# Four orders, and the skip weights as a column, in a hybrid pooling and state-space layer on one core

## The chip, the cores and the metric

The kernel runs on one core of a Trainium2 chip. The core has a matrix unit (TensorE, PE in the profile, with its weight loads as PEld), a vector engine (VectorE, DVE), a scalar engine (ScalarE, ACT), a general engine (GpSimd, POOL) and an engine that mostly issues transfers (SyncE, SP). Each works through its own instructions in program order and waits on semaphores for the others. The metric is the device time of one execution in microseconds (us), as the median of several executions.

## The reference

One layer is computed for 256 positions of a new stream and 32 positions of a running one, 288 tokens in all, in fp32. In short:

```python
def run_layer(x, pos, hist_pool, hist_sconv, h0, hist_fconv, p):
    xn = rmsnorm(x, p['norm_mix_pre'])
    proj = xn @ p['w_in']
    u, z, xbc, dt_raw = proj[..., :o1], proj[..., o1:o2], proj[..., o2:o3], proj[..., o3:]
    y_pool, new_pool = pool_mixer(u, hist_pool, pos, p['w_pool'], p['pool_scale'])
    y_ssd, new_sconv, new_h = ssd_mixer(z, xbc, dt_raw, ...)
    mix = jnp.concatenate([y_pool, y_ssd], axis=-1) @ p['w_out']
    x = x + rmsnorm(mix, p['norm_mix_post'])
    hn = rmsnorm(x, p['norm_ffn_pre'])
    up, new_fconv = causal_dwconv(hn @ p['w_up'], hist_fconv, ...)
    gate, val = up[..., :D_FF], up[..., D_FF:]
    x = x + rmsnorm((jax.nn.silu(gate) * val) @ p['w_down'], p['norm_ffn_post'])
```

The model width is 2048, the inner width of the state-space mixer 2048 (32 heads of 64), the feed-forward width 5632. Two lines of the mixer matter here. Each head adds its input times a skip weight, and the old state is carried on with the decay over all positions:

```python
    y = (y_diag + y_off).reshape(b, s, G, J, P) + D[..., None] * xh
    h = dec[..., None, None] * h + st        # dec = exp of the summed decays of a chunk
```

## The kernel before

Activations lie with channels on the 128 partitions and the 288 tokens along the free axis, so a tile of 128 channels is 128x288. The 2048 channels of the model are 16 tiles. A weight tile arrives in fp32 (`raw`); ACT copies its high part (`whi`, L152) and DVE subtracts to get the low part (`wlo`, L153). Activations are split the same way (`xn`, `hn`: ACT writes the high half, DVE the low half). A product in fp32 is then three matmuls of 128x128 by 128x288: high by high, high by low, low by high (`mm3`, L166).

The stages run one after the other on PE:

- **The first chunks** (L300 to L404). The columns of `w_in` for the B, C and first x channels are taken in 11 chunks along the contraction, six of one tile of 128 channels and five of two (CHUNKS). `prepare` splits a chunk one ahead of its use; `squares(q)` (L353 on ACT, L354 on DVE) squares two tiles of x and adds them to a running sum. The table SQUARES says behind which chunk's splits which squares are issued: `{4: (0,), 5: (1,), 6: (2,), 7: (3, 4), 8: (5,), 9: (6,), 10: (7,)}`. All of this is held in program order. In the last chunk but one, after 24 of its 36 matmuls, two matmuls by a matrix of ones (L391) sum the squares over the partitions into `prs`; from that the inverse root `rstd` is made (L394, L395), which every evacuation of these products needs.
- **The x and z projections** (L822 and on), eight and eight, each of 256 columns: 96 matmuls on PE. After an x projection the accumulators are evacuated (L442), convolved (L453, L455) and passed through tanh (L459). Meanwhile dt becomes decays `g`; `ptok` holds transposes of it by token (L567) and, from two small products, the skip weight of each channel (L575: head weights spread over the partitions by a 0/1 matrix) and the last decay of each head on all partitions (L576). Both are copied to `dcol`.
- **The masks** (`ssd_masks`): for a quad of four heads, 12 ReLU instructions (L653), one exponential (L656) on ACT, and a product with C·B (L658) on DVE. `run_masks(XS_RATE[i])` issues them after projection i; before, XS_RATE is (0, 0, 1, 0, 1, 0, 0, 1). `run_pair` then issues the products of two quads (L678 to L684), after the last x projection and after three of the z projections. L694 adds the skip term, scaled by a column of `dcol`.
- **The output projection, the new state, the residual** (L880 to L1060). The new state uses the last decays on all partitions, at L1024.
- **The residual and the up projection** (L1086 on). `rm` is the inverse root for the residual norm. Each of the 16 tiles `mg` is multiplied by it (L1119, DVE) and gets x added: tiles 0 to 7 (NEAR) from a copy in memory on chip (L1121, DVE), tiles 8 to 15 by an accumulating transfer from POOL's queue (L1123). `hn_of(t)` then makes the split `hn` (L1100 on ACT, L1101 on DVE), a square (L1108, ACT) and the running sum (L1115, DVE). The program walks s from 0 to 15 and calls `hn_of` one tile behind for near tiles and eight behind for far ones. PE takes the up projection four tiles at a time.

Between pieces that are pinned, a scheduler decides the order of each engine's instructions; it is fixed when the kernel is built.

Of the kernel before, what the change touches and what calls it, by code (L numbers as in the profile page):

```python
# [1 line left out]

# [10 lines left out]
AX = mybir.AxisListType  # L13
# [26 lines left out]
XS_RATE = (0, 0, 1, 0, 1, 0, 0, 1)  # L40
# [11 lines left out]
    ("f_b", 2 * NF), ("hist_f", 2 * 2 * NF),  # L52
# [4 lines left out]
NEAR = 8  # L57
W_GAP = 48
# [11 lines left out]
def body(  # L70
# [190 lines left out]
    hp = side1.tile([HEADS, 3], F32, name="hp")  # L261
# [26 lines left out]
    id32 = ident[:HEADS, :HEADS]  # L288
# [67 lines left out]
    SQUARES = {4: (0,), 5: (1,), 6: (2,), 7: (3, 4), 8: (5,), 9: (6,), 10: (7,)}  # L356
# [3 lines left out]
    for i, (kb, n) in enumerate(CHUNKS):  # L360
# [26 lines left out]
        for q, (r, m, k, x) in enumerate(products):  # L387
            if i == len(CHUNKS) - 2 and q == 24:
# [25 lines left out]
    act.activation(g_ssd, col["ssd_norm"], AF.Copy, scale=0.5)  # L414
    start.close()
# [30 lines left out]

    def conv_out(i, e, out):
# [11 lines left out]
        act.activation(th, c, AF.Tanh)  # L459
# [104 lines left out]
    p_t = aux([P, 10 * HEADS + NX], "ptok")  # L564
    p_tok = p_t[:, : 9 * HEADS].rearrange("p (b h) -> p b h", b=3)
# [3 lines left out]
    hv = htile("hv", NX + HEADS)  # L569
    elast = htile("elast", 1)  # L570
    act.activation(elast, g[:, 415:416], AF.Exp)
# [3 lines left out]
    follow(pe.matmul(p_[:, :NX], sel64.rearrange("h r q -> h (r q)"), hv[:, :NX], start=True, stop=True))  # L575
    follow(pe.matmul(p_[:, NX:], ones[:HEADS, :], hv[:, NX:], start=True, stop=True))  # L576
# [5 lines left out]
    dcol = const.tile([P, NX + HEADS], F32, name="dcol")  # L582
    dve.tensor_copy(dcol, p_)
# [26 lines left out]
    def ssd_first(q):  # L610
# [6 lines left out]
        act.activation(ce, gb[:, :, 384:], AF.Exp)  # L617
# [14 lines left out]
    def ssd_masks(q):  # L632
# [485 lines left out]
    for s in range(KD):  # L1118
# [5 lines left out]
        while todo and todo[0] + (1 if todo[0] < NEAR else NEAR) <= s:  # L1124
            hn_of(todo.pop(0))
# [337 lines left out]
```

## Time and profile before

| | |
|---|---|
| median of 3 runs | 1305.62 us (1305.27 to 1305.78) |
| the profiled execution | 1306.34 us |
| its span in the profile | 1304.6 us |
| x projections (PE at L166 after the first stage) | from 47.49 us |
| transposes of the decays on PE | 106.20 us |
| first products of a quad on PE | 150.45 us |
| residual norm to up projection on PE | 463.7 to 467.8 us |

The timeline gives start, duration, engine, line, and after `x` the number of instructions that a row holds; brackets give the idle time before a row and what ended it. Durations of matmuls overlap, so their pace is read from one start to the next. In the view of windows, the first columns are length and each engine's busy time with its count; at the end of the row stand PE's granted clock, the DMA share and GB/s.

### The profile page before, as it was taken

The numbers are of one execution on the slowest core, as the hardware profiler recorded it, in microseconds if no ns is written. First come the engines' busy times: TensorE is split into PE (matmuls) and PEld (weight loads), VectorE is DVE, ScalarE is ACT, GpSimd is POOL, SyncE is SP. The second block draws the span as 40 slices with busy tenths as digits, with TensorE's granted clock in tenths as the row PEclk, the third lists the DMA queues.
The fourth block names the chain that finished last, engine by engine and source line by source line (L and its number), as shares of the span: only waits on it lengthen the run. The fifth ranks groups of instructions, "written<-read, shape, count | busy, mean of one in ns | idle before, by whom it ended". The sixth has DMA issues, their size and how long they took to land.

```text
span 1304.6 us, 25289 instructions
## 1 busy us (share of the span) xinstructions
PE 1296.9 (99%) x10043; PEld 1286.6 (99%) x10043; DVE 897.0 (69%) x1531; ACT 671.6 (51%) x1013; POOL 251.7 (19%) x399
## 2 busy tenths in 40 slices
PE   9999999999999999999999999999999999999998
PEld 9999999999999999999999999999999999999997
DVE  7999987989655588867766744336666666664454
ACT  7557676646544567554544433334444454444442
POOL 2343231222222231211211100001111111201110
PEclk9999999999999999999999999999999999999999
DMA  8668877445767478766545455455545555466663
GB/s 329 204 211 274 250 242 232 137 166 169 242 213 229 140 198 259 210 185 202 172 162 166 160 170 175 157 175 182 174 162 166 175 175 165 163 233 191 209 182 113
DMA packets 110326, 251.75 MB, mean 193 GB/s; under 512 B 64768, under 2 KB 73888, under 8 KB 87936
## 3 DMA queue, kind: packets, MB, share of 16 engines
q1 hardware_dynamic: 103856, 233.36, 55.7%
q0 software_dynamic: 5824, 16.13, 4.3%
q8 instruction: 78, 1.28, 0.4%
q10 hardware_dynamic: 528, 0.66, 0.2%
q14 instruction: 40, 0.33, 0.1%
HBM read 237.11 MB, written 13.00 MB: 192 GB/s over the span
## 4 chain that ended last, share of the span: by engine, by line
PE 96%; DMA 1%; DVE 1%; ACT 1%; issue 0%; SPq 0%; ACTq 0%
PE acc L166 91%; PE acc_x L166 1%; DMA raw<-in_w_first 1%; PE py L678 1%; PE acc L1324 0%; DVE w L334 0%; PE acc L1325 0%; DMA xg<-in_x_g 0%; PE acc_t L1347 0%; DVE sq L354 0%; PE py L680 0%; PE acc_x L397 0%; PE acc L397 0%; DVE xn L321 0%; PE pst L1036 0%
## 5 line engine op out<-in xcount | busy, mean ns | idle before, releaser
L153 DVE TENSOR_TENSOR wlo<-raw,whi 128x1024 fp32r<-128x1024 f32 (+1 forms) x396 | 472.7, 1196 | 297.1 <-ACT whi L152 296.1
L152 ACT ACTIVATE whi<-raw 128x1024 fp32r<-128x1024 f32 (+1 forms) x396 | 408.0, 1033 | 471.1 <-PE acc L166 381.3
L166 PE MATMUL acc<-hn,whi 128*128 128x288 f32 x2752 | 539.0, 294 | 0.5 <-ACT hn L1100 0.4
L166 PEld LDWEIGHTS acc<-hn,whi 128*128 128x128 f32 x2752 | 436.3, 188 | 1.5 <-ACT hn L1100 0.8
L166 PE MATMUL acc<-hn,wlo 128*128 128x288 f32 x1376 | 399.6, 291 | 0.0
L166 PEld LDWEIGHTS acc<-hn,wlo 128*128 128x128 f32 x1376 | 259.0, 188 | 0.0
L166 PE MATMUL acc<-fa,whi 128*128 128x288 f32 x1320 | 257.5, 293 | 0.0
L166 PE MATMUL acc<-xn,whi 128*128 128x288 f32 x1216 | 238.5, 294 | 0.0
L166 PEld LDWEIGHTS acc<-fa,whi 128*128 128x128 f32 x1320 | 208.9, 188 | 0.0
L166 PEld LDWEIGHTS acc<-xn,whi 128*128 128x128 f32 x1216 | 192.9, 188 | 0.6 <-issue 0.5
L166 PE MATMUL acc<-fa,wlo 128*128 128x288 f32 x660 | 192.1, 291 | 0.0
L166 PE MATMUL acc<-xn,wlo 128*128 128x288 f32 x608 | 177.4, 292 | 0.0
L166 PEld LDWEIGHTS acc<-fa,wlo 128*128 128x128 f32 x660 | 124.3, 188 | 0.0
L1150 POOL COPY fc_stage<-ebuf 128x4 f32<-128x4 f32 x88 | 26.9, 306 | 472.8 <-DVE ebuf L1149 451.4
L166 PEld LDWEIGHTS acc<-xn,wlo 128*128 128x128 f32 x608 | 114.5, 188 | 0.0
L166 PE MATMUL acc<-mixs,whi 128*128 128x288 f32 x512 | 100.2, 293 | 0.0
L1145 POOL COPY ebuf<-cols 128x2 f32<-128x2 f32 x88 | 71.7, 816 | 111.1 <-DVE fc L1156 91.8
L1156 DVE SCALAR_TENSOR_TENSOR fc<-ebuf,cols,fc 128x290 f32<-128x290 f32 x176 | 90.5, 518 | 3.5 <-ACT fc L1154 0.8
L1154 ACT ACTIVATE fc<-ebuf,cols 128x290 f32<-128x290 f32 x88 | 54.4, 623 | 72.4 <-DVE ebuf L1149 72.4
L166 PEld LDWEIGHTS acc<-mixs,whi 128*128 128x128 f32 x512 | 81.1, 188 | 0.0
L166 PE MATMUL acc<-mixs,wlo 128*128 128x288 f32 x256 | 74.6, 291 | 0.0
L166 PE MATMUL acc<-mixp,whi 128*128 128x288 f32 x256 | 50.1, 293 | 0.0
(323 smaller groups left out, 1245.3 us busy)
## 6 DMA issues: line engine op xcount, KB each, us to landing
raw<-in_w_up SPq DMA_DIRECT2D x80, 1024.0 KB, 5.1
raw<-in_w_in SPq DMA_DIRECT2D x38, 1024.0 KB, 5.3
raw<-in_w_down SPq DMA_DIRECT2D x32, 1024.0 KB, 5.0
raw<-in_w_out SPq DMA_DIRECT2D x22, 1024.0 KB, 5.2
raw<-in_w_down SPq DMA_DIRECT2D x16, 768.0 KB, 4.4
raw<-in_w_up SPq DMA_DIRECT2D x14, 512.0 KB, 4.6
gb<-g_d POOLq DMA_DIRECT2D x8, 832.0 KB, 6.4
raw<-in_w_first SPq DMA_DIRECT2D x5, 768.0 KB, 13.0
```

The lines of the kernel that those rows point to most:

```text
L152: act.activation(hi, raw[:, k : k + n, :], AF.Copy)
L153: dve.tensor_tensor(lo, raw[:, k : k + n, :], hi.bitcast(F32), op=ALU.subtract)
L166: ins = pe.matmul(out, w, a[:, x, :], start=start and n == 0, stop=stop and n == 2)
L678: ins = pe.matmul(y[c, 0:256], xw[:, 0, f_], m[:, h, 0:256], start=True, stop=False)
L1145: pool.tensor_copy(e[:, 258:260], hist_f[:, :, i])
L1150: pool.tensor_copy(fc_stage[:, :, :, i], e[:, 256:324].rearrange("p (s c) -> p s c", c=34)[:, :, 0:2])
L1154: act.activation(c, e[:, 0:290], AF.Identity, bias=col["f_b"][:, i : i + 1], scale=f_w[:, 0, i : i + 1])
L1156: dve.scalar_tensor_tensor(c, e[:, r_ : r_ + 290], f_w[:, r_, i : i + 1], c, op0=ALU.mult, op1=ALU.add)
```

## The change

Four orders and one piece of data are changed.

1. SQUARES becomes `{4: (0, 1), 5: (2,), 6: (3,), 7: (4,), 8: (5,), 9: (6,), 10: (7,)}`.
2. The two matmuls of the sums are issued ahead of the last chunk instead of after 24 matmuls of the one before.
3. XS_RATE becomes (0, 0, 0, 0, 0, 1, 1, 1), and the first quad's masks and decays on ACT are issued only after the last tanh recorded so far.
4. The walk over the 16 residual tiles becomes 0, 1, 2, 3, 8, 4, 9, 5, 10, 6, 11, 7, 12, 13, 14, 15, and `hn_of` is called in it only ahead of near tiles; the rest follow at the end.
5. The skip weights come as 16 more columns of `cols` (repeated 64 times per head on the host), the last decays are stored to memory as `e_d` and read back with one broadcast to `kept`, and the two small products with all that fed them are gone. The scheduler's order of ACT, DVE and SP differs around all these places.

```diff
-XS_RATE = (0, 0, 1, 0, 1, 0, 0, 1)
+XS_RATE = (0, 0, 0, 0, 0, 1, 1, 1)
...
-    ("f_b", 2 * NF), ("hist_f", 2 * 2 * NF),
+    ("f_b", 2 * NF), ("hist_f", 2 * 2 * NF), ("skip", NX),
...
+FAR_AT = 4
...
-    SQUARES = {4: (0,), 5: (1,), 6: (2,), 7: (3, 4), 8: (5,), 9: (6,), 10: (7,)}
+    SQUARES = {4: (0, 1), 5: (2,), 6: (3,), 7: (4,), 8: (5,), 9: (6,), 10: (7,)}
...
-            if i == len(CHUNKS) - 2 and q == 24:
+            if i == len(CHUNKS) - 1 and q == 0:
...
+    skip = col["skip"]
...
-    sel = mp.tile([HEADS, 2], F32, name="sel")
-    pick = mp.tile([HEADS, NX], F32, name="pick")
-    sel64 = mp.tile([HEADS, 2, 64], F32, name="sel64")
-    with tc.issue_after(last_split[1].ins):
-        dve.tensor_reduce(sel, id32.rearrange("h (t r) -> h r t", r=2), axis=AX.X, op=ALU.add)
-        dve.tensor_reduce(pick, id32.rearrange("h (t r) -> h t r", r=2), axis=AX.X, op=ALU.add)
-        dve.tensor_copy(sel64, sel.unsqueeze(2).broadcast_to([HEADS, 2, 64]))
...
-        act.activation(th, c, AF.Tanh)
+        tanhs.append(act.activation(th, c, AF.Tanh))
...
-    hv = htile("hv", NX + HEADS)
     elast = htile("elast", 1)
     act.activation(elast, g[:, 415:416], AF.Exp)
-    dve.tensor_scalar(hv[:, 0:NX], pick, hp[:, 2:3], None, op0=ALU.mult)
-    dve.tensor_scalar(hv[:, NX:], id32, elast, None, op0=ALU.mult)
-    p_ = p_t[:, 9 * HEADS :]
-    follow(pe.matmul(p_[:, :NX], sel64.rearrange("h r q -> h (r q)"), hv[:, :NX], start=True, stop=True))
-    follow(pe.matmul(p_[:, NX:], ones[:HEADS, :], hv[:, NX:], start=True, stop=True))
+    e_d = dram.tile([HEADS, 1], F32, name="e_d")
+    sp.dma_start(out=e_d, in_=elast)
...
-    dcol = const.tile([P, NX + HEADS], F32, name="dcol")
-    dve.tensor_copy(dcol, p_)
...
-        act.activation(ce, gb[:, :, 384:], AF.Exp)
+        with ExitStack() as order:
+            if not q:
+                order.enter_context(tc.issue_after(tanhs[-1].ins))
+            act.activation(ce, gb[:, :, 384:], AF.Exp)
...
-                    if exps:
-                        order.enter_context(tc.issue_after(exps[-1].ins))
+                    order.enter_context(tc.issue_after((exps or tanhs)[-1].ins))
...
-                dve.scalar_tensor_tensor(o, o, dcol[:, t : t + 1], y, op0=ALU.mult, op1=ALU.add)
+                dve.scalar_tensor_tensor(o, o, skip[:, t : t + 1], y, op0=ALU.mult, op1=ALU.add)
...
+    kept = const.tile([P, HEADS], F32, name="kept")
+    sp.dma_start(out=kept, in_=e_d.rearrange("h o -> o h").broadcast_to([P, HEADS]))
...
-            w = dcol[:, NX:][:, heads]
+            w = kept[:, heads]
...
-    for s in range(KD):
+    turns = list(range(FAR_AT))
+    for near, far in zip_longest(range(FAR_AT, NEAR), range(NEAR, KD)):
+        turns.extend(t for t in (far, near) if t is not None)
+    for s in turns:
...
-        while todo and todo[0] + (1 if todo[0] < NEAR else NEAR) <= s:
+        while todo and todo[0] < s < NEAR:
             hn_of(todo.pop(0))
...
-    "heads": np.stack([v[n][0] for n in ("ssd_dt_bias", "ssd_a_log", "ssd_d")], axis=1),
+    "heads": np.stack([v[n][0] for n in ("ssd_dt_bias", "ssd_a_log")], axis=1),
```

How the instructions move is seen in the order of each engine's program. First PE around the sums of squares, before (`prs`, fed by `sq_r`, between rows of the last two chunks; the 16 rows of `w_dt` follow them):

```order
L397 MATMUL acc<-xn,w 128x288 x24
L391 MATMUL prs<-sq_r,ones_r 128x288 x2
L397 MATMUL acc_x<-xn,w 128x288 x12
L397 MATMUL acc<-xn,w 128x288 x24
L397 MATMUL acc_x<-xn,w 128x288 x12
L404 MATMUL acc<-xg,w_dt 32x288 x16
```

and with the change:

```order
L397 MATMUL acc<-xn,w 128x288 x24
L397 MATMUL acc_x<-xn,w 128x288 x12
L391 MATMUL prs<-sq_r,ones_r 128x288 x2
L397 MATMUL acc<-xn,w 128x288 x24
L397 MATMUL acc_x<-xn,w 128x288 x12
L404 MATMUL acc<-xg,w_dt 32x288 x16
```

The two matmuls of the sums stand twelve matmuls later. Next, PE where the decays are transposed, in the midst of the fifth x projection, before:

```order
L567 MATMUL ptok<-ident,g 128x96 x3
L575 MATMUL ptok<-hv,sel_651 128x16
L576 MATMUL ptok<-hv,ones 128x32
L597 MATMUL pcb<-bc 128x256
L598 MATMUL pcb<-bc 128x128
```

and with the change, whose lines have moved up by some numbers (L563 is the transposes, L587 the products of C and B):

```order
L563 MATMUL ptok<-ident,g 128x96 x3
L587 MATMUL pcb<-bc 128x256
L588 MATMUL pcb<-bc 128x128
L589 MATMUL pcb<-bc 128x32
L587 MATMUL pcb<-bc 128x256
```

The two rows between the transposes and the next products are gone. Last, ACT ahead of the third block of four tiles of the up projection. The rows below begin with the copy of tile 7 and the row `hn` is one copy per tile; `whi` of 1024 columns is the split of a weight block. Before:

```order
L1100 ACTIVATE hn<-mg,cols 128x288
L1108 ACTIVATE sq<-mg 128x288
L1100 ACTIVATE hn<-mg,cols 128x288
L1108 ACTIVATE sq<-mg 128x288
L152 ACTIVATE whi<-raw 128x1024
L1100 ACTIVATE hn<-mg,cols 128x288
L152 ACTIVATE whi<-raw 128x1024
L1108 ACTIVATE sq<-mg 128x288
L1100 ACTIVATE hn<-mg,cols 128x288
L152 ACTIVATE whi<-raw 128x1024
```

and with the change (L1094 is the copy, L1102 the square, L153 the split; the row of five is tiles 7 to 11, the row of two tiles 12 and 13, the next one tile 14):

```order
L1094 ACTIVATE hn<-mg,cols 128x288 x5
L1102 ACTIVATE sq<-mg 128x288
L1094 ACTIVATE hn<-mg,cols 128x288 x2
L1102 ACTIVATE sq<-mg 128x288 x3
L1094 ACTIVATE hn<-mg,cols 128x288
L153 ACTIVATE whi<-raw 128x1024
L1102 ACTIVATE sq<-mg 128x288
L153 ACTIVATE whi<-raw 128x1024
L1094 ACTIVATE hn<-mg,cols 128x288
L153 ACTIVATE whi<-raw 128x1024
```

Before, the first of these three splits stands behind the copy of tile 8 alone; now it stands behind the copies of tiles 8 to 14 and the third behind that of tile 15.

More of the change, by code (lines that the diff above doesn't have):

```diff
@@ L1 @@
 from contextlib import ExitStack
+from itertools import zip_longest
 import concourse.bass as bass
@@ L260, in body @@
     pin(sp.dma_start(out=cols, in_=cols_in))
-    hp = side1.tile([HEADS, 3], F32, name="hp")
+    hp = side1.tile([HEADS, 2], F32, name="hp")
     pin(sp.dma_start(out=hp, in_=heads_in))
@@ L445, in conv_in @@
         return e
+    tanhs = []
     def conv_out(i, e, out):
@@ L563, in body @@
     tokd = const.tile([P, 3, HEADS], F32, name="tokd")
[L564 to L565 removed]
+    p_t = aux([P, 9 * HEADS], "ptok")
+    p_tok = p_t.rearrange("p (b h) -> p b h", b=3)
     for b, go in enumerate((0, 256, MW - P)):
         follow(pe.transpose(p_tok[:, b, :], turned[:, go : go + P], ident[: 3 * HEADS, : 3 * HEADS]))
[L569 removed]
     elast = htile("elast", 1)
     act.activation(elast, g[:, 415:416], AF.Exp)
[L572 to L576 removed]
+    e_d = dram.tile([HEADS, 1], F32, name="e_d")
+    sp.dma_start(out=e_d, in_=elast)
     dve.tensor_copy(tok, p_tok[:, :, : 2 * HEADS].rearrange("p b (r h) -> p b r h", r=2))
```

4 lines of the change are left out of this document (1 added, 3 removed).

## The prediction

> **What bounds the kernel now.** I read the page's busy times first, then the chain that ended last, then a window in steady state, then what the matrix unit waited for.
>
> ```profile
> PE 1296.9 (99%) x10043; PEld 1286.6 (99%) x10043; DVE 897.0 (69%) x1531; ACT 671.6 (51%) x1013; POOL 251.7 (19%) x399
> PE 96%; DMA 1%; DVE 1%; ACT 1%; issue 0%; SPq 0%; ACTq 0%
> 600.00:800.00 200.00, 200.00 (x1540) 200.00 (x1539) 124.57 (x206) 91.40 (x122) 27.90 (x49) 1.00 0.52 170
> PE acc L166 <- ACT hn L1100: 0.4, 1, 0.4
> PE acc L397 <- DVE w L334: 0.3, 1, 0.3
> PEld prs L391 <- DVE sq_r L379: 0.3, 1, 0.3
> ```
>
> PE is busy for 99% of the span and is 96% of the chain. The window row gives its pace: 1540 matmuls in 200 us, 0.130 us each, at a granted clock of 1.00. So the time is a count of matmuls at 0.130 us plus the few places where PE stands. Those are small: the waits listed are 0.3 or 0.4 us each. What an edit gains is the PE work it takes out and the stall it takes away; what it costs is a stall it makes. Work that only moves on ACT, DVE, POOL or SP counts when it makes PE wait, and not before.
>
> **The sums of squares.** Two stalls lie in the first stage. Here are the matrix unit, ACT and DVE around the first one.
>
> ```profile
> 29.74 0.42 PE L397 MATMUL acc<-xn,w 128*128 128x288 f32 x2
> 30.41 3.20 PE L397 MATMUL acc<-xn,w 128*128 128x288 f32 x22 [0.25 <-DVE w L334]
> 25.65 0.68 ACT L353 ACTIVATE sq<-xg 128x576 f32<-128x576 f32 x1 [1.93 <-DVE sq L354]
> 26.36 0.76 DVE L354 TENSOR_TENSOR sq<-sq,sq 128x576 f32<-128x576 f32 x1 [0.75 <-ACT sq L353]
> 28.60 1.76 DVE L334 TENSOR_TENSOR w<-raw,w 128x1536 fp32r<-128x1536 f32 x1
> ```
>
> Two matmuls need 0.26 us, but 0.67 us pass from 29.74 to 30.41: 0.41 us lost, because the weights' low half is done only at 28.60 + 1.76 = 30.36. Ahead of it two squares are queued where other chunks have one; the second, at 25.65, stood 1.93 us until DVE had added the first, and the copies of the next chunk stood behind it. After the change one square stands there. The second square and its sum (0.76 us on DVE) and the 1.93 us are gone; DVE's own chain then sets it, and by these durations the low half is ready near 28.65, a microsecond before 29.74. I count the stall as gone: **-0.45** (0.41, and a little for the slower restart; 0 if another wait takes its place).
>
> ```profile
> 38.34 0.89 PE L391 MATMUL prs<-sq_r,ones_r 128*128 128x288 f32 x2
> 39.07 1.74 PE L397 MATMUL acc_x<-xn,w 128*128 128x288 f32 x12
> 38.32 0.46 DVE L379 TENSOR_TENSOR sq_r<-sq,sq_r 128x288 fp32r<-128x288 f32 x1
> 41.68 2.29 DVE L153 TENSOR_TENSOR wlo<-raw,whi 128x1024 fp32r<-128x1024 f32 x2
> ```
>
> The two matmuls of the sums take 0.73 us from 38.34 to 39.07 instead of 0.26: 0.47 lost while DVE finishes the low half at 38.78. The change puts twelve matmuls ahead of them, 1.57 us at 0.131, so PE asks at about 39.4, earlier stall already taken off. Even a DVE that gained nothing is done by then: **-0.45**. The inverse root follows later than now by what the sums move, about a microsecond. Behind it on DVE stand the splits for the next projection, done today at 43.97; from 39.07 PE still has 48 matmuls of this stage before it reads them, 6.3 us, so they have 1.4 us to spare, and **0** is counted.
>
> The price is at an earlier chunk, which now gets two squares.
>
> ```profile
> 14.33 0.52 ACT L318 ACTIVATE xn<-xg 128x288 fp32r<-128x288 f32 x1
> 16.92 1.47 ACT L330 ACTIVATE w<-raw 128x1536 fp32r<-128x1536 f32 x1
> 18.42 1.76 DVE L334 TENSOR_TENSOR w<-raw,w 128x1536 fp32r<-128x1536 f32 x1 [0.31 <-ACT w L330]
> 20.36 3.30 PE L397 MATMUL acc<-xn,w 128*128 128x288 f32 x24
> ```
>
> One more square ahead of 14.33 pushes ACT by some 0.57 us, and the low half from 20.18 to about 20.7. PE starts this chunk at 20.36 and needs the low half two matmuls later, at 20.62. I take **+0.2**, with 0 and 0.4 as ends. The next split waits for its own transfer, so the delay ends there.
>
> **The small products.** The skip weights come as a column from memory, and the last decays are written out and read back, so the products at L575 and L576 go.
>
> ```profile
> 106.45 0.32 PE ptok L575 x2
> 106.77 0.24 PE ptok L576 x2
> 96.94 0.18 ACT L571 ACTIVATE elast<-g 32x1 f32<-32x1 f32 x1
> ```
>
> They stand in the chain of waits with 0.32 and 0.24 us between matmuls that do not wait: **-0.56**. The six small DVE instructions that fed them go too; DVE is off the chain there, so they are worth nothing by themselves. The new transfers are the decays' write (32 numbers), ahead of the stores of a projection on SP's queue, and a broadcast read of 128x32 between two weight loads. The write waits for the last decays, done on ACT at 97.12, before PE's matmuls here; the read is used only in the history, two stages on. Each adds one issue to SP (0.33 us in a row further down), and behind it wait stores and loads that are fetched ahead of their use: **0**, or 0.3 each if a load behind them were just in time.
>
> **The masks of the first three quads.** They move from projections 2, 4, 7 to 5, 6, 7, and ACT starts them only after the last tanh.
>
> ```profile
> 110.97 3.72 ACT L653 ACTIVATE m<-gb,tok 128x256 f32<-128x256 f32 x12
> 116.08 1.58 ACT L656 ACTIVATE m<-m 128x1664 f32<-128x1664 f32 x1
> 118.10 1.89 DVE L658 TENSOR_TENSOR m<-m,cbt 128x1664 f32<-128x1664 f32 x1
> 144.19 1.06 ACT L152 ACTIVATE whi<-raw 128x1024 fp32r<-128x1024 f32 x1 [1.54 <-PE acc L166]
> 150.45 0.65 PE L678 MATMUL py<-m,xk 128*64 128x256 f32 x4
> 152.24 0.63 PE L678 MATMUL py<-m,xk 128*64 128x256 f32 x4
> ```
>
> PE reads the first mask at 150.45 and the second at 152.24. The first exponential would run near 136 and its DVE product near 138 to 140: ten microseconds to spare. The second stands on ACT behind the split that begins at 144.19 or a little later, because that one waits for a buffer that PE releases. So: split to 146.0, exponential to 147.6, then DVE, behind a low half and a transpose, multiplies from 148.8 to 150.7. It is needed at 152.24, so 1.6 us cover it: **0**. Behind that product DVE evacuates two accumulators up to 2.5 us later than now; they are taken again a projection later. If the cover went, each microsecond beyond would be one of PE.
>
> **The order ahead of the up projection.** This decides the sign. Tiles 8 to 15 are completed by an accumulating transfer on POOL's queue, after a product on DVE.
>
> ```profile
> 483.66 2.67 DVE L1119 TENSOR_TENSOR mg<-mg,rm 128x288 f32<-128x288 f32 x7
> 480.37 0.85 POOL L1123 DMA_DIRECT2D mg<-in_x_g  x1 [9.32 <-DVE mg L1119]
> 484.40 6.18 POOL L1123 DMA_DIRECT2D mg<-in_x_g  x7 [3.19 <-DVE mg L1119]
> 486.17 0.54 ACT L1100 ACTIVATE hn<-mg,cols 128x288 fp32r<-128x288 f32 x1 [4.95 <-DMA mg<-in_x_g]
> DMA to landing us min/median/max: 5.4/6.0/8.9
> 490.26 0.70 PE L166 MATMUL acc<-hn,whi 128*128 128x288 f32 x4
> 491.20 1.11 PE L166 MATMUL acc<-hn,whi 128*128 128x288 f32 x6
> 492.15 0.29 PE L166 MATMUL acc<-hn,wlo 128*128 128x288 f32 x1
> 492.54 1.11 PE L166 MATMUL acc<-hn,whi 128*128 128x288 f32 x4
> 493.48 0.43 PE L166 MATMUL acc_x<-hn,whi 128*128 128x288 f32 x2
> ```
>
> Today PE reaches these tiles at 490.26 and then lags: six matmuls take 0.95 us from 491.20 (0.16 too long) and four take 0.94 from 492.54 (0.42 too long), about 0.55 in all. The change sends the transfers of tiles 8 to 11 near 472, 474, 476 and 478, so they are never late. Those of 12 to 15 follow four DVE products that I place, at 0.37 us each (2.67 us for seven) and 1.2 for a split of 1024 columns (1.76 for 1536 above), at 481.6 to 483.2; the issues then run from about 482.35, half a microsecond apart.
>
> But ACT's queue changes as well. The parts of tiles 12, 13 and 14 now stand **ahead** of the split of the weights that PE needs at 490.26, and of the next, needed four matmuls later, at 490.79. ACT is free by 483.5 and stands until tile 12 lands. Then come two copies, three squares (the last behind a DVE sum and its buffer), the copy of tile 14, the split of 1.06 us, a square and the second split. From the landing to the second split's end that is 5.1 us. With the shortest landing in the row, 5.4 us, tile 12 is there at 487.75 and the second split is done near 492.85: PE loses 2.1 us and some 0.2 in two restarts, against 0.55 now, **+1.8**. If they landed early enough, nothing is lost and the 0.55 is gained. Which is nearer? Seven of the eight transfers in the row went out in one burst from 484.40, each behind the others. In the new order four go, with one weight load just ahead of them instead of two. The first, alone at 480.37, was read at 486.17: 5.8 us, with a load on each side.
>
> ```profile
> 470.19 0.86 POOL L1055 DMA_DIRECT2D ho<-hd  x1 [2.38 <-ACT ho L1050]
> 474.82 0.33 SPq L1056 DMA_DIRECT2D out<-ho  x1
> ```
>
> The nearest one with less beside it is an accumulate of the state: out at 470.19, its reader issues at 474.82, 4.6 us. I take 5.0, between 4.6 and 5.4: **+1.35**, with ends -0.55 and +2.2 (5.8 us).
>
> The Trainium skill speaks for the lower end: "DMA: Bandwidth & Descriptors", in its section on the anatomy of one DMA on the GpSimd path, fits about 2.0 us plus the bytes over 436 GB/s, which would be an estimated 2.3 us for such a tile. The row above says 5.4 at the least, so this trace does not agree for transfers beside weight loads; by the page the sum would be that of the first rival below.
>
> **The sum.** -0.45 - 0.45 + 0.2 - 0.56 + 0 + 1.35 = +0.1 us. The profiled execution took 1306.34 (span 1304.6 and 1.74 around it), 0.72 above the median of 1305.62; the profiled one would come out at 1306.4. On the median I forecast **1305.7 us: no change that can be told**, since 0.2%, about what a measurement of this kernel can tell from no change, is 2.6 us.
>
> **The rivals.** *The far tiles land in time.* Tile 12 must be there by about 485.7, 3.3 us after its issue. For it: less is queued ahead of it. Against it: no accumulate in the trace took so little. Then -0.45 - 0.45 + 0.2 - 0.56 - 0.55 = -1.8: **1303.8**, lower at most by the 0.2.
>
> *The far tiles land late, and the kernel is slower.* The two weight loads that DVE's later splits release at about 484.4 and 485 fall on the very time of the four transfers. If tiles 12 to 14 take the 8.9 us of the row's upper end, the splits come 3.5 us later than at 5.4: +1.8 + 3.5 - 1.26 = +4.0, **1309.7**. It decides from about 7.5 us to landing. For it: the last transfers of today's burst took that long. Against it: they had six before them.
>
> *The second mask is late.* DVE is in order, and everything before the product at 148.8 has waited for PE once; 1.6 us of cover are not many for a walk over 30 us. With two microseconds more on that walk and nothing else changed PE stands 0.4; with five, 3.4: **1309.1**. Against it: ACT's part of the walk is tied to buffers that PE releases, and these stay where they are.
>
> *The stalls of the first stage only move.* If the chunk with two squares now costs what the other did, -0.45 becomes 0 and 0.2 becomes 0.4: **1306.4**.
>
> **How the numbers follow.** The forecast, with the wait ahead of the up projection eating the gains: 0.45. Landing in time 0.25; landing late 0.13; the second mask late 0.08; the stalls moved 0.09. Landing in time is faster by more than 2.6 us only if a wait I have not seen also goes, 0.08, and I leave 0.03 of the forecast for the same: faster 0.11. Slower is most of landing late, 0.11, half of the mask, 0.04, and 0.03 of the rest: 0.18. No change 0.71. The range reaches from a little below the first rival to the middle between forecast and the slower ones: 1303.0 to 1308.3. The forecast's own is 1304.6 to 1306.6.
>
> **What would show it.** The two matmuls at L391 should start to start at 0.13, with no wait for DVE at chunk 8, and a gap of 0.2 near 20.6. Between the transposes at L567 and the products at L597 no other matmul. The mask's product on DVE should end near 150 and PE not wait for it at L678. In the up projection ACT should show its longest wait on the copy of tile 12, not of tile 8, and PE its wait on the split at L152 that follows: 1.5 to 2 us if I am right, none if the tiles land in time. I am wrong if PE waits anywhere else, or if its pace leaves 0.130.

## The result and the profile after

The changed kernel takes 1309.57 us (median of 7 executions, 1308.01 to 1311.34), the kernel before, beside it on the same chip, 1305.27 us (1304.76 to 1305.78). The ratio is 1.0032, with a 95% interval of 1.0021 to 1.0043: **slower by 4.3 us**. The forecast was 1305.7 in a range of 1303.0 to 1308.3.

The profiled execution of the changed kernel took 1308.94 us (span 1307.2), 0.6 below its median, while that of the kernel before was 0.7 above its own. So the two profiles are only 2.6 us apart. Below, places are read from the profiles and sizes from the medians.

First the page of the changed kernel, its busy times and the chain that ended last:

```profile
PE 1296.7 (99%) x10039; PEld 1286.7 (98%) x10039; DVE 898.6 (69%) x1525; ACT 672.2 (51%) x1013; POOL 252.7 (19%) x399
PE 95%; issue 2%; DMA 1%; ACT 1%; POOL 1%; DVE 0%; ACTq 0%; SPq 0%; POOLq 0%; DVEq 0%
```

Then what the matrix unit waited for (us in total, times, longest):

```profile
PE acc L167 <- ACT whi L153: 2.7, 2, 2.2
PE acc L167 <- ACT hn L1094: 0.4, 1, 0.4
PE acc L397 <- DVE w L334: 0.3, 1, 0.3
```

The first row is new: PE waits 2.7 us in two places for the split of a weight block. Four matmuls fewer are run and PE is busy just as long: with less to do it was slower somewhere. The page's busy times can't show that, since a matmul that is paced more slowly counts as busy.

The forecast's own places come first, on the timeline of PE in the changed kernel:

```profile
20.32 0.43 PE L397 MATMUL acc<-xn,w 128*128 128x288 f32 x2
21.05 3.14 PE L397 MATMUL acc<-xn,w 128*128 128x288 f32 x22 [0.30 <-DVE w L334]
28.70 1.72 PE L397 MATMUL acc_x<-xn,w 128*128 128x288 f32 x12
30.26 0.94 PE L397 MATMUL acc<-xn,w 128*128 128x288 f32 x6
39.63 0.43 PE L391 MATMUL prs<-sq_r,ones_r 128*128 128x288 f32 x2
39.89 1.34 PE L397 MATMUL acc<-xn,w 128*128 128x288 f32 x9
106.69 0.41 PE L563 MATMUL ptok<-ident,g 96*128 96x96 f32 x3
106.94 0.62 PE L587 MATMUL pcb<-bc 128*128 128x256 f32 x2
```

The chunk that stalled near 30 us runs through: twelve matmuls from 28.70, and the next row begins 1.56 us later. The two matmuls of the sums take 0.26 us, from 39.63 to 39.89. The price stands at 20.32: two matmuls take 0.73 us, 0.47 lost in this profile, where 0.2 was forecast. The first x projection starts at 46.75 instead of 47.49, the forecast 0.7 us earlier. Between the transposes and the products of C and B no other matmul is left.

And yet those products start at 106.94 in both kernels. An advance of 0.7 us at 47 us, and two small products fewer, have been lost on the way. The view of windows shows where, first before and then after (length; busy time and count of PE, of PEld, DVE, ACT, POOL; then PE's granted clock, the DMA share and GB/s):

```profile
60.00:75.00 15.00, 15.00 (x118) 15.00 (x117) 14.97 (x33) 7.35 (x9) 10.08 (x6) 1.00 0.68 206
75.00:90.00 15.00, 15.00 (x118) 15.00 (x117) 15.00 (x32) 7.46 (x10) 5.70 (x6) 1.00 0.63 172
```

```profile
60.00:75.00 15.00, 15.00 (x115) 15.00 (x114) 14.97 (x35) 8.11 (x11) 4.48 (x6) 1.00 0.65 194
75.00:90.00 15.00, 15.00 (x114) 15.00 (x114) 14.21 (x32) 7.14 (x9) 5.03 (x5) 1.00 0.53 157
```

In 15 us PE issues three or four matmuls fewer, without a wait and at the same granted clock of 1.00. From start to start the steady pace is 0.1333 us instead of 0.1300, from about 50 to 106 us. From 600 to 800 us both kernels have 1540 matmuls, so it is not the clock of the chip.

Last, POOL, ACT and PE of the changed kernel at the up projection, and the row of its accumulating transfers:

```profile
482.21 3.52 POOL L1120 DMA_DIRECT2D mg<-in_x_g  x4 [3.31 <-DVE mg L1116]
DMA to landing us min/median/max: 3.3/4.7/8.4
480.79 2.24 ACT L1094 ACTIVATE hn<-mg,cols 128x288 fp32r<-128x288 f32 x5
486.69 0.54 ACT L1094 ACTIVATE hn<-mg,cols 128x288 fp32r<-128x288 f32 x1 [3.33 <-DMA mg<-in_x_g]
488.94 0.54 ACT L1094 ACTIVATE hn<-mg,cols 128x288 fp32r<-128x288 f32 x1 [1.71 <-DMA mg<-in_x_g]
491.36 1.04 ACT L153 ACTIVATE whi<-raw 128x1024 fp32r<-128x1024 f32 x1
492.64 1.04 ACT L153 ACTIVATE whi<-raw 128x1024 fp32r<-128x1024 f32 x1
492.45 0.79 PE L167 MATMUL acc<-hn,whi 128*128 128x288 f32 x4 [2.16 <-ACT whi L153]
493.74 0.80 PE L167 MATMUL acc<-hn,whi 128*128 128x288 f32 x4 [0.49 <-ACT whi L153]
```

ACT copies tiles 7 to 11 from 480.79, stands for tile 12 until 486.69, and again 1.71 us for tile 13 until 488.94. Behind these two copies, three squares and the copy of tile 14 comes the split that PE wants at 490.13; it ends at 492.40. PE waits 2.16 us, then 0.49 for the next. The time from the first product on `hn` to the first on `fa` is 276.93 us before and 279.40 after.

So there are two candidates: the walk over the residual tiles, and a slow pace that no step of the forecast had. The experiments take them apart.

### The profile page after: what moved, and what is told of

It is laid out like the page before. It is cut to its first block, busy times and chain, and to the rows that moved or that the text cites. A ratio compares the mean times of both kernels' runs of the same rounds, so it can differ in the third digit from the quotient of the medians.

```text
span 1307.2 us, 25271 instructions
## 1 busy us (share of the span) xinstructions
PE 1296.7 (99%) x10039; PEld 1286.7 (98%) x10039; DVE 898.6 (69%) x1525; ACT 672.2 (51%) x1013; POOL 252.7 (19%) x399
## 4 chain that ended last, share of the span: by engine, by line
PE 95%; issue 2%; DMA 1%; ACT 1%; POOL 1%; DVE 0%; ACTq 0%; SPq 0%; POOLq 0%; DVEq 0%
PE acc L167 89%; PE acc L397 1%; DMA raw<-in_w_first 1%; PE acc_x L167 1%; PE py L670 1%; PE acc_x L397 1%; PE acc L1321 0%; DMA mg<-in_x_g 0%; PE acc L1322 0%; POOL mg L1120 0%; PE py L672 0%; PE acc_t L1344 0%; ACT w L330 0%; POOL ho L1049 0%; PE acc L404 0%
## 5 line engine op out<-in xcount | busy, mean ns | idle before, releaser
L153 ACT ACTIVATE whi<-raw 128x1024 fp32r<-128x1024 f32 (+1 forms) x396 | 408.3, 1032 | 467.4 <-PE acc L167 375.7
```

The lines of the kernel that those rows point to most:

```text
L153: act.activation(hi, raw[:, k : k + n, :], AF.Copy)
```

## The experiments

Each kernel was run beside the kernel before, whose medians lay between 1305.07 and 1305.31 us. Ratios are to it, with 95% intervals. The intervals reach about 1.2 us or more to either side, and the experiments ran in four sets, each on another chip; so smaller differences between experiments are told from the profiles and not from the times alone.

### The parts one by one

**e1_turns_back**: the changed kernel with the old walk over the residual tiles.

```diff
...
-    for s in turns:
+    for s in range(KD):
...
-        while todo and todo[0] < s < NEAR:
+        while todo and todo[0] + (1 if todo[0] < NEAR else NEAR) <= s:
```

> The changed kernel with the walk over the residual tiles as it was before, all else kept. Theory A, the stall ahead of the third block of the up projection (2.65 us in the changed kernel's trace, against 0.55 before) is the loss: the wait for the weight splits is back near 0.5 us and the median falls by 2 to 4 us, to 1305.5 to 1307.5. Theory B, the slower pace of PE in the x projections (0.1334 us a matmul from 50 to 106 us, against 0.1300) is the larger part: it falls by 2 us at most and stays 1 us or more above the kernel before. Both can hold: then 1306.0 to 1307.0 with the slow pace still in the trace.

Measured: 1305.24 us, ratio 1.0000 (0.9991 to 1.0008). The walk costs 1309.57 - 1305.24 = 4.3 us. What is left of the change is worth nothing, though its first x projection starts at 45.66. Its profile shows the slow pace, 0.1333 from 50 to 105 us.

**e2_turns_only**: the kernel before with the new walk alone (the lines above, the other way round).

> The kernel before with only the new walk over the residual tiles. Theory A: 2 to 4 us slower than before (1307.3 to 1309.3), with ACT waiting for the landing of tile 12 or 13 and PE for the two splits behind it. Theory B: at most 2.1 us slower, and the pace in the x projections stays at 0.130.

Measured: 1309.94 us, ratio 1.0034 (1.0022 to 1.0047), 4.65 us slower. From the same side, the same size. What PE waited for there, between 460 and 520 us:

```profile
PE acc L168 <- ACT whi L154: 3.0, 2, 2.5
PE acc L168 <- ACT hn L1102: 0.4, 1, 0.4
```

The x projections run at 0.1300 here. The slow pace and the walk are two things.

**e3_products_only**: the kernel before with the skip column and the decays from memory (the fifth point of the change alone).

> The kernel before with only the skip column and the decays read back, without the two small products. If the sum's term holds: 0.56 us faster (1304.7). Theory B in the form that this part brings the slow pace: the pace between 47 and 106 us reads 0.1334 and the kernel is 0.8 us slower. Otherwise the pace stays 0.130.

Measured: 1307.78 us, ratio 1.0020 (1.0011 to 1.0029): 2.5 us *slower* with two products fewer. (One of its eleven executions took 3320.58 us; it is left out of the ratio.) PE between 100 and 160 us:

```profile
PE acc L167 <- DVE wlo L154: 2.5, 3, 1.4
```

The products of C and B start at 105.70, earlier than before. But the masks stand where they were, DVE comes late with three weight splits, and the pace is 0.1333 from 127 to 150 us.

**e4_sums_only**: the kernel before with the two orders of the sums of squares.

```diff
-    SQUARES = {4: (0,), 5: (1,), 6: (2,), 7: (3, 4), 8: (5,), 9: (6,), 10: (7,)}
+    SQUARES = {4: (0, 1), 5: (2,), 6: (3,), 7: (4,), 8: (5,), 9: (6,), 10: (7,)}
...
-            if i == len(CHUNKS) - 2 and q == 24:
+            if i == len(CHUNKS) - 1 and q == 0:
```

> The kernel before with only the squares a chunk earlier and the two matmuls of the sums twelve later. If the sum's terms hold: 0.7 us faster at the first x projection (46.75 instead of 47.49) and in the median. Theory B in the form that this part brings the slow pace: the gain of 0.7 is there at 47 us and gone by 106, at 0.1334 a matmul, and the kernel is 0.5 to 0.7 us slower than before.

Measured: 1307.82 us, ratio 1.0020 (1.0011 to 1.0029), slower by 2.5 us, although the first x projection starts at 46.36, 1.1 us earlier than in the profile of before. From 48 to 106 us the pace is 0.1333. So this edit alone brings the slow pace. PE also waits 0.7 us for a low half on DVE, between 100 and 300 us.

**e5_masks_only**: the kernel before with the new XS_RATE and the order behind the last tanh.

> The kernel before with the two masks built at the changed places and nothing else of the change (the four small products stay, now behind the masks' new places). Theory (the change as a whole nets 0 without the walk, so its parts must offset one another; the products taken out alone cost 2.5 us because DVE was late with weight splits around 106 to 150 us, where the masks stood at their old places): moving the masks alone moves the second mask off that stretch, nothing else, 1305.3 +- 0.6 us, no PE wait over 0.4 us between 106 and 150. Rival (the masks at the new places collide with the first scans): a wait of 0.5 us or more before the first pair of masked products, 1306 or above.

Measured: 1305.16 us, ratio 1.0001 (0.9992 to 1.0010), with no wait of PE from 100 to 300 us. Alone the masks are worth nothing, as forecast. That they make room on DVE is seen further down: e12 has them together with the edit of e3, and the waits of e3 are gone.

### What sets the pace

PE's program in the kernels with and without the moved sums differs, in the x projections up to 104 us, at one place only. The scheduler lets two products of the second weight part go ahead of the twelve that the second accumulator takes from the first part. Here are four rows of PE's program, from the twelfth product of the first x projection on, in the kernel before, and then with the change:

```
L166 MATMUL acc<-xn,whi 128x288 x2
L166 MATMUL acc<-xn,wlo 128x288
L166 MATMUL acc<-xn,whi 128x288 x2
L166 MATMUL acc<-xn,wlo 128x288
```

```
L167 MATMUL acc<-xn,whi 128x288 x4
L167 MATMUL acc<-xn,wlo 128x288
L167 MATMUL acc<-xn,whi 128x288 x2
L167 MATMUL acc<-xn,wlo 128x288
```

The row of four holds two of the first part and the two that went ahead. The two places of PE's order that stand ahead of the forecast do not show it.

**e7_pinned**: the kernel of e1 with the products of the first x projection kept in the order in which they are written. Nothing else moves on any engine.

```diff
-        whole[0] = (FIRST_WHOLE <= groups_done[0] <= WHOLE[1]) + (groups_done[0] in WHOLE)
+        whole[0] = (groups_done[0] == 1 or FIRST_WHOLE <= groups_done[0] <= WHOLE[1]) + (groups_done[0] in WHOLE)
```

> The changed kernel with the old walk over the residual's tiles (measured 1305.24) and one thing more: the products of the first x projection are kept in the order in which the code writes them. This takes back what the recording had moved: two products of the second weight part (tile 4, upper half, of the first accumulator) that stood ahead of the twelve of the second accumulator. Theory A (the slow pace of 0.1333 us for each product from 48 to 106 us is set by that order): the pace is 0.1300 from 51 us on as in the kernel before, the products of pcb start at 105.6 +- 0.4 us instead of 106.9, and the time is 1303.8 +- 0.6 us. Theory B (the pace is set by when the projection starts, or by what else uses memory then): pace 0.1333 as before this edit, 1305.2 +- 0.6 us.

Measured: 1303.67 us, ratio 0.9991 (0.9982 to 0.9999); 1.6 us below e1. The window row of this kernel, to be read against the two pairs above:

```profile
60.00:75.00 15.00, 15.00 (x118) 15.00 (x117) 14.97 (x37) 8.40 (x11) 5.26 (x6) 1.00 0.59 170
```

118 matmuls again. The products of C and B start at 104.62, against 105.86 in e1, whose first x projection begins 0.17 us earlier, and 106.94 in the changed kernel.

**e8_two_ahead**: the kernel before with these two products put ahead by hand.

```diff
...
+                            if groups_done[0] == 1 and n_part < 2:
...
+                                    heads_.extend((m0 + m, w_, c, k, x_) for w_, x_ in pairs)
+                                if n_part == 1 and m + 1 == w // P:
+                                    early_ = heads_[:12] + heads_[24:26] + heads_[12:24] + heads_[26:]
...
+                                    for j_, w_, c_, k, x_ in early_:
+                                        pin(pe.matmul(accs[j_], w_[:, c_], acts[k][:, x_, :], start=j_ not in seen_, stop=False))
...
```

> The kernel before with the order of 24 products of the first x projection as the changed kernel has it: the two products of the second weight part ahead of the twelve of the second accumulator; the same products, nothing else moves. Theory A (that order sets the pace): 0.1333 us for each product from 51 to 106 us, the break at the turned block at 107.0 to 108.5 instead of 106.0, and 1306.7 +- 0.6 us. Theory B (the order is innocent; start time or memory sets the pace): 0.1300, 1305.3 +- 0.6 us.

Measured: 1306.33 us, ratio 1.0008 (0.9999 to 1.0017), 1.1 us more than before. Its window row:

```profile
60.00:75.00 15.00, 15.00 (x114) 15.00 (x114) 14.97 (x33) 6.99 (x9) 10.64 (x6) 1.00 0.61 182
```

The pace is 0.1333 from 50 to 106 us. The time alone can hardly be told from no change; the pace can. Taken out and put in, the order of these products decides the pace for the next 55 us: this is shown. That the time of the start or the traffic of memory sets it falls: e7 has the load of e1, and e8 that of the kernel before, and over the fourteen profiles the starts with the slow pace (45.66 to 46.83) and with the fast one (45.83 to 47.49) overlap.

**e11_sums_pinned**: e4 with the written order kept, as in e7.

> The kernel before with the sums of squares moved (which alone measured 1307.82) and the products of the first x projection kept in written order. Theory (the sums gain some 0.7 us in the first stage, as the starts of the first x projection in twelve profiles show: mean 46.98 with the old sums, 46.28 with the new; the loss came from the pace that the recorded order set): pace 0.1300 from 51 to 104 us, 1304.6 +- 0.7 us. Rival (the sums' move costs elsewhere too: the block of turned rows stands some 16 products later in PE's order, and its readers start later): pace 0.1300 but 1305.6 or above, with the later pairs of masked products shifted by 1 us or more.

Measured: 1306.89 us, ratio 1.0013 (1.0004 to 1.0022). The order gives the pace back, 0.1300 up to 132 us, but not the time: the theory's 1304.6 falls and the rival's figure holds. PE waits here, between 100 and 300 us, and behind the wait near 134 us its pace is 0.1333 up to 148:

```profile
PE acc L166 <- DVE wlo L153: 1.4, 2, 0.7
```

The turned block (the transposes and the products of C and B) stands later in PE's program, the masks are at their old places, and the second pair of quads starts at 181.21 instead of 179.32. In e7, with the masks moved and the small products gone as well, these waits are absent; which of the two removes them is not shown, since no run moves the sums and the masks alone.

**e12_no_sums**: e7 with the sums of squares where the kernel before has them.

> The kernel of e7 (1303.67) with the sums of squares left where the kernel before has them: the masks moved, the four small products gone, the old walk, the written order of products. Theory (the two products of 0.28 us each were on TensorE's path, and with the masks moved nothing takes their place): 0.56 us below the kernel before, 1304.7 +- 0.6 us, with the first product of pcb 0.3 us or less behind the first turned block instead of 0.9, and no wait over 0.4 us between 106 and 150 us. Rival (the splits wait on VectorE there again, as with the products gone and the masks at their old places): a wait of 1 us or more, 1306 or above.

Measured: 1304.45 us, ratio 0.9995 (0.9986 to 1.0004), 0.62 us below its own runs of before, with no wait of PE between 100 and 300 us. That agrees with 0.56 us for the products once the masks have moved, though the time alone can't tell it from nothing. The profile can: the products of C and B start 0.25 us behind the transposes, where the kernel before takes 0.90. The sums bring e7 a further 0.8 (1304.45 to 1303.67), which is inside the intervals too; in the profiles the first x projection starts at 46.33 us in the mean of the eight with the new sums and at 47.00 in that of the six with the old.

### What the walk costs

**e6_far1**: the changed kernel with the far tiles sent from the second step on.

```diff
-FAR_AT = 4
+FAR_AT = 1
```

> The changed kernel with one number different: the far tiles begin to alternate after one near tile instead of four, so tiles 12 to 15 are issued some 3 to 4 us earlier on the GpSimd queue and still in the order far, near. Theory (the stall of 2.7 us at the first up projection's second half, and the 1.3 us after it, come from tiles 12 and 13 landing after 486 us): both stalls go, hn to fa falls from 279.4 to 276.5, and the time is 1305.3 +- 0.8 us (4 us below the changed kernel); the first product on hn may start 0.3 to 0.6 us later. Rival (the alternation itself delays the near tiles, or the eight accumulates share the transfer engines with the weight loads so that the last ones land at the same time whatever their issue): a stall of 2 us or more stays somewhere in the first up projection, 1308 or above.

Measured: 1309.02 us, ratio 1.0028 (1.0018 to 1.0038). A miss. Seven tiles go out by 478.88 and are on time. The eighth is behind DVE's splits:

```profile
483.05 0.86 POOL L1120 DMA_DIRECT2D mg<-in_x_g  x1 [3.32 <-DVE mg L1116]
488.81 0.54 ACT L1094 ACTIVATE hn<-mg,cols 128x288 fp32r<-128x288 f32 x1 [3.32 <-DMA mg<-in_x_g]
```

One late tile is enough, because all the copies now stand ahead of the splits of the third quarter. PE waits 1.7 us for two of these splits.

That the landing alone isn't it is seen in e1, with the old walk. ACT there:

```profile
485.31 0.54 ACT L1094 ACTIVATE hn<-mg,cols 128x288 fp32r<-128x288 f32 x1 [5.31 <-DMA mg<-in_x_g]
486.09 1.05 ACT L153 ACTIVATE whi<-raw 128x1024 fp32r<-128x1024 f32 x1
488.39 0.54 ACT L1094 ACTIVATE hn<-mg,cols 128x288 fp32r<-128x288 f32 x1 [1.26 <-DMA mg<-in_x_g]
488.83 1.05 ACT L153 ACTIVATE whi<-raw 128x1024 fp32r<-128x1024 f32 x1
```

ACT waits for its tiles even longer, 5.31 and 1.26 us, and PE waits for no split. Between the copies stand the splits, so each is done as ACT comes by.

**e10_splits_behind**: e7 with one wait more, so that the splits of the third quarter follow the copy of tile 13 (`behind_13` holds that copy and is given to the up projection as `held`).

```diff
...
-                parts = split_w(raw, kb, n, w, tuple(wait) + ((after or ()) if m0 else ()) + (hold if i else tail if m0 + w // P == n_all else ()))
+                parts = split_w(raw, kb, n, w, tuple(wait) + ((after or ()) if m0 else ()) + (hold + (tuple(held) if i == 2 else ()) if i else tail if m0 + w // P == n_all else ()))
...
+        if t == 13:
+            behind_13.append(hi)
...
```

> The kernel of e7 (old walk, measured 1303.67) with one wait more: the four weight splits of the third quarter of the first up projection come after the normalisation of tile 13 on ScalarE, where the recording of the changed kernel has them, and not between those of tiles 8 to 12. The tiles are issued and land as in e7. Theory (the order on ScalarE is what costs, and the walk moved it): PE waits 3 to 6 us for these splits, 1307 to 1310 us. Rival (the times of landing, and not what is queued behind them, made the difference between the walks): under 1 us of waits, 1303.7 to 1304.7.

Measured: 1311.34 us, ratio 1.0045 (1.0033 to 1.0058), 7.7 us above e7 and 1.3 above the upper end of what was expected. ACT and PE:

```profile
484.58 0.54 ACT L1095 ACTIVATE hn<-mg,cols 128x288 fp32r<-128x288 f32 x1 [5.64 <-DMA mg<-in_x_g]
487.93 0.54 ACT L1095 ACTIVATE hn<-mg,cols 128x288 fp32r<-128x288 f32 x1 [2.47 <-DMA mg<-in_x_g]
491.70 0.52 ACT L1095 ACTIVATE hn<-mg,cols 128x288 fp32r<-128x288 f32 x1
492.13 3.46 ACT L153 ACTIVATE whi<-raw 128x1024 fp32r<-128x1024 f32 x4
493.22 1.57 PE L167 MATMUL acc<-hn,whi 128*128 128x288 f32 x5 [5.09 <-ACT whi L153]
```

The tiles go out as in e7, seven in one burst. ACT reads tiles 8 and 9 at 484.58 and 487.93, in e7 at 483.54 and 487.76. What stands behind them on ACT has changed: the four splits run at 492.13, where e7 has them from 484.67 on, and PE waits 5.09 us. (The low halves on DVE, and the products from 493.22 on, are in another order too; they come behind that wait.) From the first product on `hn` to the first on `fa` it takes 7.2 us longer than in e7; what is more than the wait is lost in the next 24 products, most of which start 0.240 us apart. So the order on ACT is what costs, with the first landings within 1.1 us of what they were: this is shown.

These slow products show a second part of the cost, PE's clock. In three profiles the granted clock falls to 0.50 behind the stall: for 3.4 us in e2 and in e6, for 6.8 us in e10. Products then start 0.240 us apart instead of 0.130. In the profile of the changed kernel it stays at 1.00. Here are the same two microseconds in the changed kernel, e2 and e10:

```profile
495.00:497.00 2.00, 2.00 (x18) 2.00 (x17) 2.00 (x3) 1.25 (x4) 0.00 (x0) 1.00 0.82 246
495.00:497.00 2.00, 2.00 (x10) 2.00 (x10) 2.00 (x4) 0.97 (x3) 0.00 (x0) 0.50 0.75 252
495.00:497.00 2.00, 2.00 (x11) 2.00 (x10) 2.00 (x3) 2.00 (x6) 0.00 (x0) 0.50 0.76 213
```

From the first product on `hn` to the first on `fa`, the walk costs 2.9 us at full clock (279.40 in the changed kernel, 276.47 in e1), and 4.6 with the fall (281.50 in e2, 276.93 before), though PE waits only 0.3 us longer in e2: thirteen products at 0.240 are 1.4 us. Of the other executions only the mean granted clock is on record. The changed kernel's seven have 0.997 to 0.999, and the fastest two are at 0.999; the eleven of e1 have 0.999 or 1.000. In e6 five executions at 0.999 took 1307.29 to 1309.32 us, and three at 0.998 took 1309.94 to 1310.80. So most executions of the changed kernel probably lost clock at this stall; that is inferred, since no trace of them is on record.

**e9_far0**: the changed kernel with the walk begun by a far tile (FAR_AT = 0) and the order of e7.

```diff
-FAR_AT = 4
+FAR_AT = 0
```

> The changed kernel, the products of the first x projection kept in written order (as in e7), and the walk over the residual begun with a far tile: 8, 0, 9, 1, ... 15, 7, so that tile 15 is issued near 477 us and not 483. In the recorded order ScalarE then has all eight far normalisations in one run ahead of the weight splits of the third quarter. Theory (what costs is ScalarE standing at a tile that has not landed, with weight splits queued behind it; the landing takes 3.3 to 6 us): all tiles have landed when ScalarE reaches them near 482 us, its wait on the landing and PE's waits on the splits go, hn to fa is 276.5 +- 0.5 us, and the time is 1304.1 +- 0.8 us (0.4 us later start of the stage than with the old walk). Rival (the alternation itself starves the first products on hn, because VectorE comes to each near tile 0.4 us later): PE waits on hn in the first 15 us of the stage for 1 us or more in all, 1305.5 or above.

Measured: 1305.35 us, ratio 1.0001 (0.9992 to 1.0010). The last transfer goes out at 478.30, and ACT comes to its tile, the last of nine copies, some 6 us later:

```profile
478.30 0.87 POOL L1120 DMA_DIRECT2D mg<-in_x_g  x1 [1.17 <-DVE mg L1116]
```

ACT then waits for no tile, PE loses 0.57 us at the splits, and the stage takes 277.4 us, against 277.06 in e7. The stall is gone, as the theory has it; the stage begins 0.4 us later, behind one more product on DVE. The time missed the upper end of what was expected by 0.45 us, and the stage by 0.4. In the two profiles the rest of the difference to e7 lies at the very start: the first x projection begins at 46.93 here and at 45.83 in e7, with the same program up to there. That start varies from 45.66 to 46.93 in the eight profiles with the new sums; what makes it vary was not tried.

## Why the prediction was wrong

Point by point, by its own steps:

- **The sums of squares** (-0.45, -0.45, +0.2): right in sum for the first stage. -0.7 was forecast; 0.74 is seen in this pair of profiles, 0.67 between the means of all, and 0.8 between e12 and e7. The price at the earlier chunk was 0.47 in the profile of the changed kernel, but it runs from 0 (e7, e10, e11) to 0.51 (e1) in the eight with the new sums, so +0.2 was a fair middle. What the step left out lies behind the first stage: alone the edit loses 2.5 us (e4), and with the pace given back still 1.8 (e11), in waits for DVE.
- **The small products** (-0.56): in line with e12's 0.62 and with the 0.65 us by which the products of C and B come closer to the transposes. But that is so only with the masks moved; alone the edit loses 2.5 us (e3). The step costed it alone, with DVE "off the chain there".
- **The masks** (0): right, both alone (e5) and in the changed kernel:

```profile
148.12 1.85 DVE L650 TENSOR_TENSOR m<-m,cbt 128x1664 f32<-128x1664 f32 x1
150.36 0.65 PE L670 MATMUL py<-m,xk 128*64 128x256 f32 x4
152.15 0.63 PE L670 MATMUL py<-m,xk 128*64 128x256 f32 x4
```

  The second mask's product ends at 149.97, 2.2 us ahead of its use, where 1.6 was forecast. The rival of a late mask did not come.
- **The order ahead of the up projection** (+1.35): this step failed, by its size. The instructions are the ones it named: ACT stands at the copy of tile 12, and PE waits for the splits behind it. Measured 4.3 (after against e1) and 4.65 (e2). Two things are missing from its term. First, it took only tile 12 as late: "Then come two copies", with no wait in between. Tile 12 was even earlier than assumed, 4.5 us after its issue and not 5.0; but tile 13 kept ACT another 1.71 us, and from the landing of tile 12 to the end of the second split it was 7.0 us instead of 5.1. The ends, -0.55 and +2.2, were both made from the one tile and left this out. In the profiled execution, at full clock, this comes to 2.5 us against the kernel before and 2.9 against e1. Second, it had no term for the clock: where the stall is followed by a granted clock of 0.50, as in the profiles of e2 and e6, some 1.4 us come on top, and the medians of 4.3 and 4.65 fit that. What decides whether the clock falls is open: in e6 it fell behind waits of 1.2 and 0.5 us, in the profile of the changed kernel it didn't behind 2.2 and 0.5. The rival "the far tiles land late" came near the result with +4.0 in all, but by luck: it needed some 7.5 us for tile 12, which took 4.5. It was put at 0.13.
- **The pace** (not a term): +1.6 us, from e1 to e7. The forecast named it among the things that would prove it wrong. The reason was to be found in PE's order, in the first products after the moved sums; the change's text doesn't touch that place, and the forecast took its order to be as before.

Two readings of the forecast were short without bearing on its sum. Its list of waits leaves out the two longest, 1.3 us at L300 and 0.7 at L1389, at the very start and end of the kernel (1.3 and 1.0 after the change). And from 39.07 PE has not only 48 matmuls ahead of the next projection but also the narrow ones of L404, from 45.42 to 47.49, so the splits had about 3.5 us to spare and not 1.4.

Together: the first stage and the products gain 1.6 us (e7), the pace takes 1.6 back (e1), and the walk adds 4.3. That is the measured +4.3. e7 is the version that beats both kernels, by 1.6 us against the one before in the medians (by the interval of the ratio, 0.1 to 2.3): the sums, the masks and the column of the change, the old walk, and the first products in written order.

The rule of the Trainium skill that the forecast weighed, in "DMA: Bandwidth & Descriptors", its section on the anatomy of one DMA on the GpSimd path, would give an estimated 2.3 us for such a tile. The landings of the changed kernel were 3.3 us at the least and 8.4 at the most, so this trace does not agree with it here either.

## What to carry to other kernels

When an engine works in order, price a reordering by what stands *behind* each instruction that may wait, and take every one of the late arrivals into the sum, not the first alone: here much the same waits on transfers cost next to nothing or 7 us, by the place of four weight splits. A stall of the matrix unit can also cost more than its own length, when the granted clock falls behind it (e2, e6, e10). Parts of a change are to be costed together where they share an engine: three that lose 2.5 us or gain nothing alone gained 1.6 us together, with the order of products held. And compare the whole order of the busiest engine, not only where the edit points: two products moved by the scheduler took back all that three edits had won.

## What was not expected of the hardware

A stream of like matmuls (128x128 weights, 288 columns, each with its own weight load) has two steady paces at a granted clock of 1.00: 0.1300 us, a cycle of six starts in 0.780 us, and 0.1333 us, six in 0.800. Each repeats an uneven pattern of its own for over 50 us, through changes of tile and weights, until a break in the stream. Which of the two it is was set in the x projections by the order of 14 products at the start (e7, e8). In e3 and e11 the slow pace also sets in behind a wait for a weight split (127 to 150 and 134 to 148 us). Why that order leads to the one or the other is open: no experiment went further.

The Trainium skill, "TensorE: Matmul & The Clock Gate", in its section on the back-to-back issue gap, gives the spacing of isolated warm matmuls, in ns, as the columns over 2.4 plus about 2.5, an estimated 122.5 ns for 288 columns; for a stream of pairs of weight load and matmul it says that both set the spacing, with about 81 ns at 128 columns and 131 at 512. Both paces of this trace, 130.0 and 133.3 ns, lie above the formula and near the page's value for 512 columns, and the page has one value for a size where the trace shows two.
